# A hybrid GLA and retention trunk on one Trainium2 core: 64 and 16 bytes of slack behind each k-tile of the two activation tiles

## The chip, the cores and the metric

The kernel runs on one core of one Trainium2 chip. The metric is the device time of one execution in microseconds; smaller is better.

## What is computed

Two decoder layers on 256 tokens of width 2048, in float32: first gated linear attention (GLA, 4 heads), then multi-scale retention (8 heads). Each has a pre-RMSNorm, a wide input projection, a chunked mixer, a SiLU gate, an output projection and a residual add; a final RMSNorm ends it. Cut to the matrix work:

```
h = x
h = h + gla(rms_norm(h) )       # proj = hn @ w_in  (2048 x 10240), out = (o * silu(gate)) @ w_out (4096 x 2048)
h = h + retention(rms_norm(h))  # proj = hn @ w_in  (2048 x 12288), out = (o * silu(gate)) @ w_out (4096 x 2048)
return rms_norm(h, final_norm)
```

Nearly all the work is these four projections. Their weights, 60 groups of 2048 x 512 numbers, are read from HBM once.

## The kernel before

**Tiles.** A contraction of 2048 is cut into 16 k-tiles of 128, one k-tile on the 128 partitions. Two tiles hold activations for all 16 k-tiles: `xhl`, the normalized tokens, and `ogt`, the gated mixer outputs (half of 4096 at a time). Both have the shape `[P, NKT, 2, SEQ]`: partition, k-tile, high or low part, 256 tokens. Float32 products are made from three products of rounded numbers (high x high, high x low, low x high), so each activation and each weight is kept as a rounded high part and a rest. In a partition, one k-tile is a row of 2 x 256 x 4 = 2048 bytes, and the rows lie one behind the other.

**Weights.** `emit_raw` loads four k-tiles of a group into `raw`; `emit_split` makes the high part `hi` on ScalarE (L151) and the rest `lo` on VectorE (L152), two k-tiles at a time, two steps ahead of TensorE (`LOOK = 2`). Three buffers of `raw`, `hi` and `lo` each go round.

**Matmuls.** TensorE has a stationary operand of 128 x 128, which is loaded by a LDWEIGHTS before each matmul, and a moving operand of up to 512 columns. Two helpers use the activation tiles in two ways:

```python
def mm3(ps, lhs, kt, t, hi, lo, q):                       # in group_x: L184, L185, L186
    xh = lhs[:, kt, 0, t * P : (t + 1) * P]
    xl = lhs[:, kt, 1, t * P : (t + 1) * P]
    mm(ps, xh, hi[:, q, :], start=kt == 0, stop=False)
    mm(ps, xh, lo[:, q, :], start=False, stop=False)
    mm(ps, xl, hi[:, q, :], start=False, stop=kt == NKT - 1)
...
                    mm(ps[c], wh, rhs[:, kt, :, :], start=kt == 0, stop=False)               # in group_w: L219
                    mm(ps[c][:, 0, :], wl, rhs[:, kt, 0, :], start=False, stop=False)        # L220
```

- `group_x` (48 of the 60 groups and the tail): the activations are **stationary** (128 tokens of `xhl` or `ogt`, 512 bytes of a partition), the weights move, 512 columns. Six matmuls use one k-tile, then the next k-tile follows. Outputs named `gv`, `gg`, `rv`, `rg` read `xhl`; `ga`, `gb`, `ra`, `rb` and `tail` read `ogt`.
- `group_w` (12 groups, `gqk` and `rqk`): the weights are stationary and a row of `xhl` **moves**, 512 columns for the high weights (L219, L217) and 256 for the rest (L220, L216). Eight matmuls use one k-tile.
- In the last group (`tail`, half columns of 256), the high weights are written into the k-tile rows of `xhl`, which is no longer needed.

A few other matmuls come between: `zps` (L369, the stationary operand is 48 columns of `wa1`, whose k-tiles lie 192 bytes apart), `dg` (L507, the stationary operand is `ones_r`), `rs` (L809 to L811), `o_mms` and transposes. The order on each engine is the program's order as a scheduler at build time puts it; small work of the mixers (`side`) is fed in between the weight steps.

**Addresses.** All tiles lie in one list per partition. `smalls` is padded to 96 numbers and `ones` to 88, so that before the change `resid`, `xhl`, `ogt`, `trig`, `raw`, `hi`, `lo`, `v` and the other large working tiles start at multiples of 512 bytes, and so does every slice of them that a large matmul reads. `ones_r` is an exception: it starts 160 bytes past such a multiple.

Of the kernel before, what the change touches and what calls it, by code (L numbers as in the profile page):

```python
# [11 lines left out]
F32R = mybir.dt.float32r  # L12
# [5 lines left out]
P = 128  # L18
SEQ = 256
D = 2048  # L20
EPS = 1e-6
NKT = D // P
# [33 lines left out]
def kernel(  # L56
# [38 lines left out]
    def const(shape, name, dtype=F32):  # L95
        return one.tile(shape, dtype, tag=name, name=name)
# [152 lines left out]
    sm = const([P, 96], "smalls")[:, 0:S_N]  # L249
    ident = const([P, P], "ident")  # L250
    resid = const([P, 2, D], "resid")
    xhl = const([P, NKT, 2, SEQ], "xhl", F32R)
    ogt = const([P, NKT, 2, SEQ], "ogt", F32R)
    trig = const([P, 2, SEQ], "trig")
    rr = const([P, 2, 2], "rr")
    r2_ = const([P, 2, 2], "r2")
# [735 lines left out]
```

## Time and profile before

| | |
|---|---|
| median of 2 runs | 1416.12 us (1416.04 to 1416.2) |
| the profiled execution: its time, its span | 1417.53 us, 1415.8 us |
| TensorE matmul, weight load (share of the span) | 1403.9 us (99%), 1180.0 us (83%) |
| VectorE, ScalarE, GpSimd | 908.6 us (64%), 690.4 us (49%), 46.1 us (3%) |
| mean granted TensorE clock | 0.997 |

The span runs from the first instruction to the last one; the execution's own time is 1.73 us longer. Matmuls are pipelined: the profile gives each one a time from its start to its modelled end (389 ns for most with 512 columns), and the next one starts before that end. What counts for the total is the distance from one start to the next, which is read from the start times of a timeline. In the profile, PE is the matmul row and PEld the weight load.

### The profile page before, as it was taken

What the parts mean: (1) busy time and instruction counts of PE and PEld (TensorE: products, weight loads), DVE (VectorE), ACT (ScalarE), POOL (GpSimd) and SP (SyncE); (2) the same over time, 40 slices, a digit from 0 to 9 for tenths busy, and PEclk for the clock granted to TensorE, in tenths of its full rate; (3) what the DMA queues carried; (4) which work ended last, traced back from release to release, by engine and by line L of the source; (5) the groups of instructions that cost most, each with busy time, mean ns of one, the idle gap of its engine ahead of it and who ended that gap; (6) DMA issues with size and microseconds to landing.
All of it is one profiled execution on the core that took longest, in us unless ns stands there. A gap on an engine that the chain in (4) does not pass through costs nothing.

```text
span 1415.8 us, 17504 instructions
## 1 busy us (share of the span) xinstructions
PE 1403.9 (99%) x6800; PEld 1180.0 (83%) x6800; DVE 908.6 (64%) x1430; ACT 690.4 (49%) x889; POOL 46.1 (3%) x98
## 2 busy tenths in 40 slices
PE   8999999999999999999999999999999999999997
PEld 6888888888888888888888888888888888888887
DVE  6685796545845774665766666665556666666664
ACT  3665655534555655554444444444334444444453
POOL 0001020000010020000000000000000000000000
PEclk9999999999999999999999999999999999999999
DMA  8654555555555555555555555555555555555662
GB/s 287 240 177 149 192 180 175 183 204 180 177 179 178 188 189 179 178 178 183 190 194 192 194 189 198 179 199 181 203 182 184 196 184 199 182 203 176 209 212 94
DMA packets 40499, 266.72 MB, mean 188 GB/s; under 512 B 4880, under 2 KB 5392, under 8 KB 9696
## 3 DMA queue, kind: packets, MB, share of 16 engines
q1 hardware_dynamic: 37536, 257.57, 53.9%
q0 software_dynamic: 2160, 6.95, 1.5%
q8 instruction: 53, 0.87, 0.2%
q10 hardware_dynamic: 720, 1.09, 0.2%
q14 instruction: 30, 0.25, 0.0%
HBM read 263.49 MB, written 2.10 MB: 188 GB/s over the span
## 4 chain that ended last, share of the span: by engine, by line
PE 99%; DMA 0%; SPq 0%; DVE 0%; ACT 0%; issue 0%
PE rqk_ps L219 8%; PE gv_ps L184 4%; PE gg_ps L185 4%; PE rv_ps L184 4%; PE gv_ps L185 4%; PE gv_ps L186 4%; PE rv_ps L185 4%; PE rv_ps L186 4%; PE gg_ps L186 4%; PE gg_ps L184 4%; PE rg_ps L184 4%; PE rg_ps L185 4%; PE rg_ps L186 4%; PE rqk_ps L220 4%; PE gqk_ps L219 4%; PE gb_ps L184 2%
## 5 line engine op out<-in xcount | busy, mean ns | idle before, releaser
L152 DVE TENSOR_TENSOR lo<-raw,hi 128x1024 fp32r<-128x1024 f32 (+1 forms) x473 | 576.6, 1222 | 420.7 <-ACT hi L151 419.9
L151 ACT ACTIVATE hi<-raw 128x1024 fp32r<-128x1024 f32 (+1 forms) x473 | 499.5, 1057 | 614.4 <-PE rg_ps L186 104.6
L219 PE MATMUL rqk_ps<-xhl,hi 128*128 128x512 f32 x480 | 166.9, 398 | 0.0
L220 PE MATMUL rqk_ps<-xhl,lo 128*128 128x256 f32 x480 | 126.4, 280 | 0.0
L219 PEld LDWEIGHTS rqk_ps<-xhl,hi 128*128 128x128 f32 x480 | 88.8, 188 | 17.5
L185 PE MATMUL gg_ps<-lo,xhl 128*128 128x512 f32 x256 | 100.5, 393 | 0.0
L185 PE MATMUL gv_ps<-lo,xhl 128*128 128x512 f32 x256 | 100.4, 392 | 0.0
L185 PE MATMUL rv_ps<-lo,xhl 128*128 128x512 f32 x256 | 100.4, 392 | 0.0
L186 PE MATMUL gv_ps<-hi,xhl 128*128 128x512 f32 x256 | 100.3, 392 | 0.0
L186 PE MATMUL gg_ps<-hi,xhl 128*128 128x512 f32 x256 | 100.0, 391 | 0.0
L186 PE MATMUL rv_ps<-hi,xhl 128*128 128x512 f32 x256 | 99.7, 389 | 0.0
L185 PE MATMUL rg_ps<-lo,xhl 128*128 128x512 f32 x256 | 99.6, 389 | 0.0
L186 PE MATMUL rg_ps<-hi,xhl 128*128 128x512 f32 x256 | 99.6, 389 | 0.0
L184 PE MATMUL gv_ps<-hi,xhl 128*128 128x512 f32 x256 | 93.1, 391 | 0.0
L184 PE MATMUL rv_ps<-hi,xhl 128*128 128x512 f32 x256 | 92.1, 390 | 0.0
L220 PEld LDWEIGHTS rqk_ps<-xhl,lo 128*128 128x128 f32 x480 | 89.1, 189 | 3.4
L184 PE MATMUL rg_ps<-hi,xhl 128*128 128x512 f32 x256 | 91.8, 389 | 0.0
L184 PE MATMUL gg_ps<-hi,xhl 128*128 128x512 f32 x256 | 91.8, 391 | 0.0
L219 PE MATMUL gqk_ps<-xhl,hi 128*128 128x512 f32 x240 | 81.2, 406 | 1.6 <-ACT hi L151 1.6
L220 PE MATMUL gqk_ps<-xhl,lo 128*128 128x256 f32 x240 | 57.9, 283 | 0.5 <-DVE lo L152 0.5
L186 PEld LDWEIGHTS rv_ps<-hi,xhl 128*128 128x128 f32 x256 | 48.1, 188 | 10.0
L186 PEld LDWEIGHTS rg_ps<-hi,xhl 128*128 128x128 f32 x256 | 48.0, 188 | 10.0
(265 smaller groups left out, 2381.8 us busy)
## 6 DMA issues: line engine op xcount, KB each, us to landing
raw<-in_w_all SPq DMA_DIRECT2D x238, 1024.0 KB, 4.9
resid<-in_x_n SPq DMA_DIRECT2D x2, 1024.0 KB, 8.0
gg<-in_gn_g POOLq DMA_DIRECT2D x8, 256.0 KB, 3.8
gb<-in_gn_b POOLq DMA_DIRECT2D x8, 256.0 KB, 4.5
dm<-in_dmat POOLq DMA_DIRECT2D x8, 192.0 KB, 2.6
raw<-in_w_all SPq DMA_DIRECT2D x4, 256.0 KB, 5.0
raw<-in_w_all SPq DMA_DIRECT2D x2, 512.0 KB, 7.4
xt<-in_x_t SPq DMA_DIRECT2D x2, 512.0 KB, 8.5
```

The source lines that it names most:

```text
L151: nc.scalar.activation(hi[:, sl], src[:, sl], AF.Copy)
L152: nc.vector.tensor_tensor(lo[:, sl], src[:, sl], hi[:, sl].bitcast(F32), ALU.subtract)
L184: mm(ps, xh, hi[:, q, :], start=kt == 0, stop=False)
L185: mm(ps, xh, lo[:, q, :], start=False, stop=False)
L186: mm(ps, xl, hi[:, q, :], start=False, stop=kt == NKT - 1)
L219: mm(ps[c], wh, rhs[:, kt, :, :], start=kt == 0, stop=False)
L220: mm(ps[c][:, 0, :], wl, rhs[:, kt, 0, :], start=False, stop=False)
```

## The change

Each k-tile's row of `xhl` gets 64 bytes behind it (its stride grows from 2048 to 2112 bytes), each row of `ogt` 16 bytes (2064), and an unused tile of 256 bytes follows `ogt`:

```diff
-    xhl = const([P, NKT, 2, SEQ], "xhl", F32R)
-    ogt = const([P, NKT, 2, SEQ], "ogt", F32R)
+
+    def tokens(name, slack):
+        t = const([P, NKT, 2 * SEQ + slack], name, F32R)
+        return t[:, :, 0 : 2 * SEQ].rearrange("p k (a t) -> p k a t", a=2)
+
+    xhl = tokens("xhl", 16)
+    ogt = tokens("ogt", 4)
+    const([P, 64], "fill")
```

In the built program `xhl` starts at byte 33792 of the partition as before, `ogt` moves from 66560 to 67584, and all tiles behind it move by 1024 + 256 + 256 = 1536 bytes, three times 512: their place in a 512-byte block is what it was. So k-tile `k` of `xhl` starts 64k bytes, and that of `ogt` 16k bytes, past a multiple of 512 where both were at 0.

No instruction is added, removed or moved on any engine. The lines below the edit have numbers higher by 6. Only the splits of the last weights change their form, as they write two rows of `xhl` that no longer touch. On ScalarE, near the end of the program, the splits of weights (`hi` or `xhl` from `raw`) stand before as

```order
L151 ACTIVATE hi_10865<-raw_10767 128x1024
L151 ACTIVATE xhl<-raw_10847 128x1024 x2
L151 ACTIVATE hi_10883<-raw_10813 128x1024
L151 ACTIVATE hi_10899<-raw_10813 128x1024
L151 ACTIVATE xhl<-raw_10881 128x1024 x2
L151 ACTIVATE xhl<-raw_10915 128x1024 x2
```

and after as

```order
L151 ACTIVATE hi_10866<-raw_10768 128x1024
L151 ACTIVATE xhl<-raw_10848 128x2x512 x2
L151 ACTIVATE hi_10884<-raw_10814 128x1024
L151 ACTIVATE hi_10900<-raw_10814 128x1024
L151 ACTIVATE xhl<-raw_10882 128x2x512 x2
L151 ACTIVATE xhl<-raw_10916 128x2x512 x2
```

The rows are the same and in the same places; the 1024 numbers of one split become two runs of 512.

## The prediction

> **What bounds the kernel now.** First the page: the busy shares, the granted clock, and the chain of work that ended last.
>
> ```profile
> span 1415.8 us, 17504 instructions
> ...
> PE 1403.9 (99%) x6800; PEld 1180.0 (83%) x6800; DVE 908.6 (64%) x1430; ACT 690.4 (49%) x889; POOL 46.1 (3%) x98
> ...
> PEclk9999999999999999999999999999999999999999
> ...
> PE 99%; DMA 0%; SPq 0%; DVE 0%; ACT 0%; issue 0%
> ```
>
> The chain is TensorE from end to end at full clock; no DMA and no other engine ends a wait that matters. The time is the sum of the distances between matmul starts, so only what changes these distances counts. Next the groups of instructions by line, on PE, for how many matmuls of each kind there are:
>
> ```profile
> L219 PE MATMUL rqk_ps<-xhl,hi 128*128 128x512 f32 x480 | 166.9, 398 | 0.0
> L220 PE MATMUL rqk_ps<-xhl,lo 128*128 128x256 f32 x480 | 126.4, 280 | 0.0
> L185 PE MATMUL gg_ps<-lo,xhl 128*128 128x512 f32 x256 | 100.5, 393 | 0.0
> L185 PE MATMUL gb_ps<-lo,ogt 128*128 128x512 f32 x128 | 50.2, 392 | 0.0
> L185 PE MATMUL rb_ps<-lo,ogt 128*128 128x512 f32 x96 | 37.4, 389 | 0.0
> L185 PE MATMUL tail_ps<-tail,ogt 128*128 128x256 f32 x64 | 18.1, 283 | 0.0
> ```
>
> With `xhl` stationary there are four outputs (gv, gg, rv, rg) on three lines of 256, 3072 matmuls; with `ogt` stationary three of 3 x 128 and one of 3 x 96, 1440; the tail has 192. With `xhl` moving there are 12 groups of 64 + 64: 768 of 512 columns and 768 of 256. These 6240 of 6800 read the two changed tiles.
>
> Now the distances, from the timeline of PE (start, length, line). First a stretch of `ra`, the first and last row, with the counts of its three lines between them:
>
> ```profile
> 973.76 0.62 PE L184 MATMUL ra_ps<-hi,ogt 128*128 128x512 f32 x2
> ...
> 995.52 0.39 PE L184 MATMUL ra_ps<-hi,ogt 128*128 128x512 f32 x1
> ```
> ```profile
> L186 PE MATMUL ra_ps<-hi,ogt 128*128 128x512 f32 x32 | 12.4, 389 | 0.0
> L185 PE MATMUL ra_ps<-lo,ogt 128*128 128x512 f32 x32 | 12.4, 389 | 0.0
> L184 PE MATMUL ra_ps<-hi,ogt 128*128 128x512 f32 x32 | 11.2, 389 | 0.0
> ```
>
> 96 matmuls in 995.52 - 973.76 = 21.76 us: **226.7 ns** each, every one with the same 389 ns length. I call this the steady beat. The tail does the same with 256 columns:
>
> ```profile
> 1399.84 0.28 PE L185 MATMUL tail_ps<-tail,ogt 128*128 128x256 f32 x1
> ...
> 1401.88 0.28 PE L184 MATMUL tail_ps<-xhl,ogt 128*128 128x256 f32 x1
> ```
>
> 17 steps (a row each 0.12 us) in 2.04 us, 120 ns. The 256 columns more cost 226.7 - 120 = 106.7 ns, so 512 columns stream in 213.3 ns and each matmul has 13.3 ns on top, whatever its length. This excess is the only thing that an address could change.
>
> **Is the excess a collision of the weight load with the moving operand?** Look at a matmul beside which no weight load ran (timelines of PEld and of PE):
>
> ```profile
> 59.81 0.19 PEld L184 LDWEIGHTS gg_ps<-hi,xhl 128*128 128x128 f32 x1
> 60.35 0.33 PEld L395 LDWEIGHTS rb<-dg,ones 128*16 128x16 f32 x4 [0.35 <-issue]
> ```
> ```profile
> 60.04 0.39 PE L184 MATMUL gg_ps<-hi,xhl 128*128 128x512 f32 x1
> ```
>
> It streamed from 60.04 on; the next load began 0.31 us later, yet its length is 0.39 us as ever. So in the steady beat the loads cost the stream hardly anything: the aligned addresses are already without collisions, and staggering them has little to take away. Lengths track distances, and over the whole run they hardly go below the steady ones (the answers by source line, min/median/max ns):
>
> ```profile
> L184 PE MATMUL gg_ps<-hi,xhl x256: 387/389/476, 58.0 to 579.5; 128*128 128x512 f32 x128
> L219 PE MATMUL rqk_ps<-xhl,hi x480: 387/395/477, 670.9 to 1270.9; 128*128 128x512 f32 x160
> L220 PE MATMUL rqk_ps<-xhl,lo x480: 274/280/285, 671.4 to 1271.1; 128*128 128x256 f32 x160
> ```
>
> With `xhl` stationary the median sits 2 ns above the minimum; with `xhl` moving, 395 and 280 stand 8 and 6 above.
>
> **What a stationary address off the 512-byte grid costs.** Two places of this run show it. `dg` loads `ones_r`, 160 bytes off the grid, four times:
>
> ```profile
> 75.14 0.40 PE L186 MATMUL gg_ps<-hi,xhl 128*128 128x512 f32 x1
> 75.38 0.64 PE L507 MATMUL dg<-qkp,ones_r 128*128 128x256 f32 x4
> 75.86 0.62 PE L184 MATMUL gg_ps<-hi,xhl 128*128 128x512 f32 x2
> ...
> 77.25 0.39 PE L184 MATMUL gg_ps<-hi,xhl 128*128 128x512 f32 x1
> ```
>
> The matmul beside which the first such load runs takes 0.24 us, the four of 256 columns 0.12 each, and the six that follow 77.25 - 75.86 = 1.39 us, 232 ns each, before the beat is back. From 75.14 to 77.25 it is 2.11 us where the steady beat makes 7 x 0.2267 + 4 x 0.12 = 2.07: some 0.04 us for two changes of address, there and back, about **20 ns a change**. And `zps` steps its stationary address by 192 bytes each time:
>
> ```profile
> 21.23 2.94 PE L369 MATMUL zps<-xhl,wa 128*48 128x512 f32 x12
> 24.02 0.62 PE L219 MATMUL gqk_ps<-xhl,hi 128*128 128x512 f32 x2
> ```
>
> Twelve in 2.79 us, 232.5 ns: with a step each time the beat is never found, 5.8 ns a matmul.
>
> But a break needs no odd address: one matmul of another length does it too, with all operands on the grid.
>
> ```profile
> 705.47 0.28 PE L809 MATMUL rs<-rqs,rks 128*128 128x256 f32 x1
> 705.58 0.63 PE L184 MATMUL rv_ps<-hi,xhl 128*128 128x512 f32 x2
> ...
> 706.97 0.39 PE L184 MATMUL rv_ps<-hi,xhl 128*128 128x512 f32 x1
> ```
>
> 0.11 us, then six in 1.39: 1.50 against 0.12 + 6 x 0.2267 = 1.48, again 0.02 us lost. So the beat is a rhythm that TensorE falls into and that any irregular step breaks for about six matmuls.
>
> The Trainium skill speaks against any effect: in "TensorE: Matmul & The Clock Gate", section "Step-by-step: what each phase is for", it gives TensorE two independent read ports, so that loading the next weights takes nothing from the running matmul. By that rule the sum is zero and the time 1416.1 us. The trace agrees in the steady beat (0.39 us with and without a load) and disagrees beside `ones_r` (0.24 us instead of 0.2267).
>
> **The sum.** No instruction is added or moved; the eight splits of changed form run on ScalarE, 49% busy, under the tail's matmuls, and cost nothing unless they doubled: one takes about as long as any other split,
>
> ```profile
> L151 ACT ACTIVATE xhl<-raw 128x1024 fp32r<-128x1024 f32 x8 | 8.0, 1052 | 4.3 <-DMA raw<-in_w_all 4.3
> ```
>
> and eight more microseconds of ScalarE would still fit there. What remains is the break at each new k-tile of the stationary operand: 32 groups x 16 = 512 steps of 64 bytes on `xhl`, 15 x 16 = 240 of 16 bytes on `ogt`. No row here has a step of 16 or 64 bytes under 128-column loads. Bounds: nothing (each such step is absorbed), or 20 ns each, 752 x 0.02 = 15 us, and if the beat is never found again, 5.8 ns x 4512 = 26 us. Below nothing: the minima allow 2 ns x 4512 = 9 us, and 8 x 768 + 6 x 768 ns = 11 us where `xhl` moves, since there the rows are off the beat now and the new residues may put them on it; all together 20 us.
>
> The nearest row is the 160-byte one, and I scale its price with the size of the step, an estimate: 20 x 64/160 = 8 ns x 512 = 4.1 us, and 20 x 16/160 = 2 ns x 240 = 0.5 us; for `xhl` moving, tail and the rest, zero between their ends. The sum is +4.6 us on the profiled execution's 1417.53, which lies 1.41 above the median: 1417.53 + 4.6 - 1.41 = 1420.7 us, **1421**. That is +0.3%; a run of this kernel tells about 2% from no change for a verdict.
>
> **The rivals.**
> - *No effect*, 1416 us: steps in whole 64 or 16 bytes keep the phase. For it: the beat is the same at all multiples of 512. Chance 0.20.
> - *The beat is lost*, the slower side: a 64-byte step counts as much as `ones_r`'s. Place: each first matmul of a k-tile in gv, gg, rv, rg. Price between 15 us (a break each) and 26 us (never found, as in `zps`): 1431 to 1442, say 1436. It decides from the point where six matmuls, one k-tile's worth, don't suffice to find the beat. Against it: `zps` has 48-column loads and stood off the beat before. Chance 0.19.
> - *The stagger helps*: rows where `xhl` moves fall nearer their minima, and stationary ones gain 1 to 2 ns: half of the 20 us to all of it, 1396 to 1406, say 1404. For it: L219's 395 against 387. Against it: nothing in the trace shows a new residue doing that. Chance 0.19.
> - *The 13.3 ns are themselves a collision that staggering ends*: taking half of it from 4512 + 1536 matmuls saves 6.65 x 6048 = 40 us, 1376. Against it: the matmul without a load. Chance 0.05. The same page of the skill, in "Back-to-back issue gap", has N/2.4 + 2.5 ns for a warm matmul, an estimate of 215.8 ns here; no run here shows it, 226.7 is measured.
>
> **How the numbers follow.** The forecast, a small loss or none to speak of (1417 to 1428), has 0.37; with the rivals that is 1. Range: the largest part of both middle rivals, 1398 to 1440. Faster by over 2% (below 1387.8): the fourth rival and a little of the third, 0.06. Slower by over 2% (above 1444.4): what lies beyond the second one's end, if moving rows get worse too, 0.05. Within: 0.89.
>
> **What would show it.** In the profile after: the stretch of `ra` at 226.7 ns a matmul and 389 ns on every row says that 16-byte steps are absorbed; a median of gv, gg, rv, rg above 389, or maxima of 395 to 398 every six matmuls, that 64-byte steps break the beat; near 395 throughout, that it is lost. L219 and L220 below 395 and 280 is the third rival. All medians well under 387 would make the prediction wrong: then loads and stream do collide at equal residues. An unchanged profile at another time, or a span lost outside PE, would make it wrong in another way.

## The result, and the profile after

The changed kernel takes **1436.54 us** (median of 2 runs, 1435.76 to 1437.32) against 1416.12 us: a ratio of 1.0144, with a 95% interval of 1.0101 to 1.0188. It is slower by some 20 us, 1.4%, and the whole interval lies above 1. The profiled execution took 1437.32 us. All times below are medians over a kernel's executions; one execution far out of line, 3659.68 us of the first experiment's kernel, moves that median from 1441.56 to 1441.72 us and is left out of its ratio.

First the page of the changed kernel: span, busy shares, granted clock, and the chain that ended last.

```profile
span 1435.5 us, 17504 instructions
...
PE 1423.0 (99%) x6800; PEld 1181.0 (82%) x6800; DVE 909.8 (63%) x1430; ACT 690.4 (48%) x889; POOL 45.4 (3%) x98
...
PEclk9999999999999999999999999999999999999999
...
PE 99%; DMA 0%; ACT 0%; SPq 0%; DVE 0%; issue 0%; ACTq 0%
```

The chain is TensorE from end to end as before, at the same clock, with as many instructions on every engine. The span grew by 1435.5 - 1415.8 = 19.7 us, PE's busy time by 1423.0 - 1403.9 = 19.1 us; the other engines moved by about 1 us or less. The time went into the matmuls themselves. The groups by line show which (PE rows; the last two numbers ahead of the idle time are busy us and mean ns):

```profile
L219 PE MATMUL rqk_ps<-xhl,hi 128*128 128x512 f32 x480 | 167.1, 397 | 0.0
L220 PE MATMUL rqk_ps<-xhl,lo 128*128 128x256 f32 x480 | 126.9, 281 | 0.0
L185 PE MATMUL gg_ps<-lo,xhl 128*128 128x512 f32 x256 | 101.6, 397 | 0.0
```

Where `xhl` moves, nothing happened in sum: 397 and 281 ns, 398 and 280 before. Where it is stationary, as in `gg`, a matmul is 4 ns longer: 397 against 393. The two answers below are for one of the three `mm3` lines (L186), first of the kernel before, then of the changed one; the columns are minimum, median and maximum ns, and the first and last start.

```profile
L186 PE MATMUL rg_ps<-hi,xhl x256: 389/389/389, 717.8 to 1318.2; 128*128 128x512 f32 x128
L186 PE MATMUL rb_ps<-hi,ogt x96: 389/389/479, 1319.1 to 1385.6; 128*128 128x512 f32 x96
```
```profile
L186 PE MATMUL rg_ps<-hi,xhl x256: 388/394/398, 728.1 to 1337.0; 128*128 128x512 f32 x128
L186 PE MATMUL rb_ps<-hi,ogt x96: 387/394/479, 1337.9 to 1405.7; 128*128 128x512 f32 x96
```

Before, all 256 matmuls of `rg` on this line had 389 ns, the steady beat without an exception. After, the median is 394 in both, so the 16-byte steps on `ogt` cost as much per matmul as the 64-byte steps on `xhl`.

The timeline of PE in the changed kernel shows where in `ra` the beat is lost (start, length; six matmuls use one k-tile, counted from the group's beginning; the residue is the place of the stationary address past a multiple of 256 bytes, and the weights are at 0):

```profile
976.59 0.63 PE L184 MATMUL ra_ps<-hi,ogt 128*128 128x512 f32 x2
...
977.99 0.39 PE L184 MATMUL ra_ps<-hi,ogt 128*128 128x512 f32 x1
...
986.34 0.39 PE L184 MATMUL ra_ps<-hi,ogt 128*128 128x512 f32 x1
...
987.70 0.62 PE L184 MATMUL ra_ps<-hi,ogt 128*128 128x512 f32 x2
...
990.19 0.40 PE L186 MATMUL ra_ps<-hi,ogt 128*128 128x512 f32 x1
990.43 0.62 PE L184 MATMUL ra_ps<-hi,ogt 128*128 128x512 f32 x2
...
991.82 0.40 PE L184 MATMUL ra_ps<-hi,ogt 128*128 128x512 f32 x1
```

- From 976.59 to 977.99 the k-tile at residue 128: six matmuls in 1.40 us, 233 ns each. It doesn't settle within the k-tile.
- From 986.34 the k-tile at 240, from 987.70 the one at 0 (the next group begins), then the one at 16 up to 990.19: 17 matmuls in 3.85 us, 226.5 ns. **Through two steps of 16 bytes the beat holds.**
- The matmul at 990.19 still has a stationary operand at residue 16, yet takes 0.24 us. What runs beside it is the load of the next one, the first at residue 32. From 990.43 on, at 32, six take 1.39 us, 232 ns.

The same holds over all of `ga`, `gb`, `ra` and `rb`: by the starts in PE's timeline, the k-tiles at residues 240, 0 and 16 take 226.8, 227.5 and 228.4 ns a matmul on average, the other thirteen 229.6 to 233.7 (where the next matmul of the same output starts within 300 ns).

So it seems to be the load running beside a matmul whose address counts, and what counts need not be that the address has changed: some residues keep the beat and others don't. That leaves three theories. **A, the difference:** a matmul is on the beat when the load beside it and its own moving operand stand at nearly the same place modulo 256 bytes. **B, the step** (the prediction's): any change of residue breaks the beat for some six matmuls. **C, the grid:** addresses off the 512-byte grid are slow in themselves.

### The profile page after: what moved, and what is told of

Same layout as the page of the kernel before. It is cut to its first block, busy times and chain, and to the rows that moved or that the text cites. A ratio compares the mean times of both kernels' runs of the same rounds, so it can differ in the third digit from the quotient of the medians.

```text
span 1435.5 us, 17504 instructions
## 1 busy us (share of the span) xinstructions
PE 1423.0 (99%) x6800; PEld 1181.0 (82%) x6800; DVE 909.8 (63%) x1430; ACT 690.4 (48%) x889; POOL 45.4 (3%) x98
## 4 chain that ended last, share of the span: by engine, by line
PE 99%; DMA 0%; ACT 0%; SPq 0%; DVE 0%; issue 0%; ACTq 0%
PE rqk_ps L219 8%; PE gg_ps L185 4%; PE gv_ps L184 4%; PE rv_ps L184 4%; PE gv_ps L185 4%; PE rg_ps L185 4%; PE rv_ps L185 4%; PE gg_ps L184 4%; PE rg_ps L184 4%; PE rv_ps L186 4%; PE gv_ps L186 4%; PE rg_ps L186 4%; PE gg_ps L186 4%; PE rqk_ps L220 4%; PE gqk_ps L219 4%; PE gb_ps L184 2%
## 5 line engine op out<-in xcount | busy, mean ns | idle before, releaser
L186 PE MATMUL gv_ps<-hi,xhl 128*128 128x512 f32 x256 | 101.3, 396 | 0.0
L186 PE MATMUL gg_ps<-hi,xhl 128*128 128x512 f32 x256 | 101.0, 395 | 0.0
L186 PE MATMUL rv_ps<-hi,xhl 128*128 128x512 f32 x256 | 100.8, 394 | 0.0
L186 PE MATMUL rg_ps<-hi,xhl 128*128 128x512 f32 x256 | 100.7, 393 | 0.0
L185 PEld LDWEIGHTS rg_ps<-lo,xhl 128*128 128x128 f32 x256 | 48.1, 188 | 11.3
L186 PEld LDWEIGHTS rg_ps<-hi,xhl 128*128 128x128 f32 x256 | 48.2, 188 | 11.0
```

## The experiments

Each diff is against the kernel before, cut to the lines that matter; `tokens` is the function that the change brings in. Where a tile behind is pushed, padding brings the tiles behind it to the grid again unless the diff says otherwise.

**Both token tiles shifted by 128 bytes, no step.**

```diff
+    const([P, 32], "ahead")
     xhl = const([P, NKT, 2, SEQ], "xhl", F32R)
     ogt = const([P, NKT, 2, SEQ], "ogt", F32R)
+    const([P, 96], "behind")
```

> No slack, so no k-tile differs from another; both token tiles as a whole stand 128 bytes off the 512-byte grid, the weights on it. Theory A (what counts is where the stationary address stands against the moving one, modulo 256 bytes; steps don't matter): all 4512 matmuls with xhl or ogt stationary go as those of residue 128 do in the changed kernel, where the rows of ra alternate 229 and 238 ns: 4512 x about 6.5 ns = +29 us, 1445 us, slower than the staggered kernel. Theory B (a change of residue breaks the beat for some six matmuls, as the prediction had it): there is no change, the beat holds at 226.7 ns, 1416 us. Theory C (every address off the 512-byte grid is slow in itself): 1445 us as A.

Measured: 1441.72 us, ratio 1.0174 (1.0154 to 1.0195). No k-tile differs from another, and the loss is 25.3 us where the stagger lost 20.4 (the intervals of the two ratios overlap). L186 by source line:

```profile
L186 PE MATMUL rg_ps<-hi,xhl x256: 390/392/404, 729.7 to 1341.3; 128*128 128x512 f32 x128
L186 PE MATMUL rb_ps<-hi,ogt x96: 390/393/478, 1342.3 to 1410.3; 128*128 128x512 f32 x96
```

The minimum is 390: of these 256 matmuls of `rg` not one has the 389 ns of the beat. Theory B alone is out. The size is 25.3 us and not the 29 expected: over 4512 matmuls that is 5.6 ns each, where the rows of `ra` had suggested 6.5.

**The weights shifted by 128 instead of the token tiles.**

```diff
     ogt = const([P, NKT, 2, SEQ], "ogt", F32R)
+    const([P, 32], "fill")          # everything behind: 128 bytes off the grid
```

> No slack; the token tiles on the grid, the split weights and all tiles behind them 128 bytes off it. Theory A (the difference counts, whichever side is shifted): as with the token tiles shifted by 128 alone, about 1445 us. Theory B (steps): 1416 us. A theory by which only the stationary address counts: 1416 us.

Measured: 1443.11 us, 1.0183 (1.0166 to 1.0200), with the same lengths:

```profile
L186 PE MATMUL rg_ps<-hi,xhl x256: 390/393/405, 731.2 to 1342.9; 128*128 128x512 f32 x128
```

Here every stationary token slice is on the grid. So it isn't the stationary address alone. Which side is shifted doesn't matter at 128 bytes, where ahead and behind are the same modulo 256.

**Everything shifted by 128.**

```diff
+    const([P, 32], "ahead")
     sm = const([P, 96], "smalls")[:, 0:S_N]
```

> No slack; 128 bytes ahead of all large tiles, so that token tiles and weights stand off the 512-byte grid by the same 128 bytes. Theory A (stationary against moving): the difference is zero again, beat 226.7 ns, 1416 us. Theory B (steps): 1416 us. Theory C (off the grid is slow in itself): as with the token tiles alone, 1445 us.

Measured: 1416.41 us, 1.0000 (0.9991 to 1.0009).

```profile
L186 PE MATMUL rg_ps<-hi,xhl x256: 389/389/389, 716.0 to 1316.4; 128*128 128x512 f32 x128
```

Both operands are off the grid and the beat is there for all 256. Theory C is out; the difference counts.

**Steps of 256 bytes.** Residues 0 and 256 modulo 512 in turn (even k-tiles, slack, odd k-tiles):

```diff
+    class Tokens:                       # k-tile kt at [kt % 2][kt // 2]
+            t = const([P, 2, NKT // 2 * 2 * SEQ + 64], name, F32R)
...
+            return self.v[(p, kt // 2, kt % 2, *rest)]
+    xhl = Tokens("xhl")
+    ogt = Tokens("ogt")
```

> The k-tiles of both token tiles alternate between residues 0 and 256 modulo 512: the even ones lie together, then 256 bytes of slack, then the odd ones. Theory A (modulo 256): 256 counts as zero, the beat holds through every step, 226.7 ns, 1416 us. Theory B (each of 752 steps breaks the beat, 20 ns each): +15 us, 1431 us. Theory A with a period of 512 bytes instead: half of the k-tiles off the beat, +13 to +15 us, 1430 us.

Measured: 1416.04 us, 0.9996 (0.9987 to 1.0005).

```profile
L186 PE MATMUL rg_ps<-hi,xhl x256: 389/389/389, 716.0 to 1316.4; 128*128 128x512 f32 x128
```

752 steps of 256 bytes cost nothing, and every matmul of `rg` on this line has 389 ns as before: 256 bytes count as zero, 128 don't, so the period is 256 bytes, and a change of address as such breaks no beat.

The Trainium skill, "TensorE: Matmul & The Clock Gate", section "Step-by-step: what each phase is for", says that the load has a read port of its own and takes no read bandwidth from the running matmul. By that rule these four runs would agree; they lie 27 us apart and differ in addresses alone, so here the measurement decides. What inside the chip has the period of 256 bytes no run shows.

**The two slacks apart.**

```diff
+    xhl = tokens("xhl", 16)      # 64 bytes; the other run: 0
+    ogt = tokens("ogt", 0)       # the other run: 4, 16 bytes
```

> Only the 64-byte slack on xhl; ogt as before. The prediction's sum: 8 ns x 512 steps, +4.1 us, 1420 us. Theories A and B alike, by the rows of the changed kernel (gv, gg, rv, rg 231.4 to 231.6 ns instead of 226.7 to 227.5, 3072 matmuls): +13 us, 1429 us, and ga, gb, ra, rb back at 226.7 ns.

> Only the 16-byte slack on ogt; xhl as before. The prediction's sum: 2 ns x 240 steps, +0.5 us, 1416.6 us. By the rows of the changed kernel (231.4 ns instead of 226.9, 1440 matmuls): +6.5 us, 1422.6 us. Together with the run that has the slack on xhl alone it should add up to the whole change, +20 us.

Measured: 1429.40 us, 1.0091 (1.0076 to 1.0106), with the slack on `xhl`; 1422.15 us, 1.0040 (1.0025 to 1.0055), with that on `ogt`. Against the 1416.22 us beside them that is +13.2 and +5.9, together +19.1 of the change's +20.4. L186 of the first run and then of the second:

```profile
L186 PE MATMUL rg_ps<-hi,xhl x256: 388/394/398, 723.4 to 1330.5; 128*128 128x512 f32 x128
L186 PE MATMUL rb_ps<-hi,ogt x96: 387/389/479, 1331.4 to 1398.0; 128*128 128x512 f32 x96
```
```profile
L186 PE MATMUL rg_ps<-hi,xhl x256: 389/389/389, 720.1 to 1322.2; 128*128 128x512 f32 x128
L186 PE MATMUL rb_ps<-hi,ogt x96: 387/394/479, 1323.1 to 1390.9; 128*128 128x512 f32 x96
```

Of the outputs with stationary tokens, each slack hits those that read its own tile and no others. A step costs 13.2 / 512 = 26 ns with 64 bytes and 5.9 / 240 = 25 ns with 16.

**A quarter of the step on xhl.**

```diff
+    xhl = tokens("xhl", 4)       # 16 bytes
+    ogt = tokens("ogt", 0)
```

> Slack on xhl alone, 16 bytes instead of 64: residues 0, 16, ... 240. The prediction's price in proportion to the step: 2 ns x 512, +1 us, 1417 us. Theory A (the residue against the weights counts, 3 of 16 residues keep the beat): 3072 x (231.4 - 227.0) = +13.5 us, 1429.6 us, as much as 64-byte steps. Theory B (each step breaks it): 512 x 20 ns = +10 us, 1426 us.

Measured: 1431.13 us, 1.0102 (1.0087 to 1.0117): 14.9 us, with 16-byte steps no less than with 64-byte ones.

**How wide is the window? A constant 16 and a constant 240 bytes.**

```diff
+    def shifted(name):
+        t = const([P, NKT * 2 * SEQ + 64], name, F32R)
+        t = t[:, 4 : 4 + NKT * 2 * SEQ]        # 16 bytes; the other run: 60, 240 bytes
+        return t.rearrange("p (k a t) -> p k a t", a=2, t=SEQ)
...
+    xhl = shifted("xhl")
+    ogt = shifted("ogt")
```

Each tile grows by 256 bytes, so `ogt` starts at another 256 past the grid in both runs; modulo 256 the two tiles agree.

> No slack; both token tiles as a whole stand 16 bytes off the grid. Theory A, with the window that the changed kernel's ra rows show (beat held at 240, 0 and 16, lost at 32): 1416 us, 226.7 ns. Theory B: 1416 us. Theory C: anything from 1416 us (in proportion to the offset) to 1445 us.

Measured: 1433.03 us, 1.0114 (1.0099 to 1.0129). This was a miss, since all three residues had held the beat in the rows of `ra` above. L186 again, three outputs:

```profile
L186 PE MATMUL rg_ps<-hi,xhl x256: 390/395/398, 725.8 to 1333.2; 128*128 128x512 f32 x128
L186 PE MATMUL ga_ps<-hi,ogt x128: 394/394/397, 255.2 to 345.2; 128*128 128x512 f32 x128
L186 PE MATMUL ra_ps<-hi,ogt x128: 389/389/483, 963.1 to 1050.3; 128*128 128x512 f32 x128
```

`ga` and `ra` are the same work on the same tile at the same residue. `ra` is mostly on the beat, and `ga` never is on this line: its minimum is 394. At 16 bytes two rhythms can go on. PE's timeline of this run shows one change from the beat to the other:

```profile
708.55 0.39 PE L184 MATMUL rv_ps<-hi,xhl 128*128 128x512 f32 x1
...
709.91 0.62 PE L184 MATMUL rv_ps<-hi,xhl 128*128 128x512 f32 x2
710.36 0.60 PE L813 MATMUL rs<-ra 128*128 128x128 f32 x4
...
711.04 0.40 PE L186 MATMUL rv_ps<-hi,xhl 128*128 128x512 f32 x1
...
712.44 0.39 PE L184 MATMUL rv_ps<-hi,xhl 128*128 128x512 f32 x1
```

Before the four small matmuls of `rs`, six take 709.91 - 708.55 = 1.36 us, 227 ns each; after them, six take 712.44 - 711.04 = 1.40 us, 233 ns each, and `rv` doesn't come back. In this run every change from one rhythm to the other that lasts five matmuls or more stands next to matmuls of another output; in between, the rhythm stays what it was. So what came before decides which one a group is in; what in it decides isn't shown. I looked at the other side next:

> As the run at 16 bytes, with the token tiles as a whole at residue 240 (16 bytes short of 256) against the weights. Both residues held the beat in the rows of ra of the changed kernel, but at a constant 16 the beat held in ra (226.7 ns) and was lost in rg (233.3). Theory: the window is one-sided; 240 also brings a lost beat back (rows of 240 follow those of 224 in the changed kernel at 226.9 ns): gv, gg, rv, rg at 227 ns, 1414 to 1418 us. Rival: the window is symmetrical, and 240 loses it in part like 16, 1430 us.

Measured: 1418.51 us, 1.0016 (1.0007 to 1.0025).

```profile
L186 PE MATMUL rg_ps<-hi,xhl x256: 389/389/390, 719.4 to 1321.0; 128*128 128x512 f32 x128
L186 PE MATMUL ga_ps<-hi,ogt x128: 387/392/397, 254.3 to 342.5; 128*128 128x512 f32 x128
L186 PE MATMUL ra_ps<-hi,ogt x128: 387/390/478, 953.7 to 1041.3; 128*128 128x512 f32 x128
```

Here `rg` is on the beat throughout. `ga` and `ra` are not, but they lose little. A group of 96 in `ra`, from its first row to the next group's first:

```profile
997.67 0.62 PE L184 MATMUL ra_ps<-hi,ogt 128*128 128x512 f32 x2
...
1019.59 0.62 PE L184 MATMUL ra_ps<-hi,ogt 128*128 128x512 f32 x2
```

That is 21.92 us, 228.3 ns a matmul, 1.6 above the beat; a group of `ga` at 16 bytes (278.23 to 300.63 in that run's timeline) took 233.3. The window is one-sided: a stationary address 16 bytes behind the moving one costs a seventh of one 16 bytes ahead (2.3 us against 16.6). Of the constant differences tried, 0, 16, 128 and 240, only 0 was without loss.

**The stagger kept, the weights staggered with it.** 32 bytes on `xhl`, and the split weights start at the residue of their k-tile:

```diff
+            step = 0 if i // NSUB in OUT else 8
+            off = i % NSUB * SUB * step % 64
...
+                t = pool.tile([P, SUB * GW + 64], F32R, tag=tag, name=f"{tag}{i}")
+                t = t[:, off : off + SUB * (GW + step)] if step else t[:, 0 : SUB * GW]
...
+    xhl = tokens("xhl", 8)
```

> The stagger kept and its harm taken out: 32 bytes of slack on xhl, and the split weights of every group that works with xhl start at the same residue as their k-tile, so that within a k-tile stationary and moving address always agree modulo 256; ogt without slack. Only the load of a new k-tile's first weights runs beside the last matmul of the old k-tile, 32 bytes apart. Theory A: the beat returns within each k-tile; 512 steps at nothing to 20 ns, 1416 to 1426 us, below the 1429 to 1431 us of unmatched slack on xhl alone. Theory that the steps themselves cost: 1429 us or more, as without the match.

Measured: 1425.60 us, 1.0063 (1.0046 to 1.0079); its kernel before took 1417.48. One k-tile of `rg` and the first row of the next in PE's timeline:

```profile
864.83 0.62 PE L191 MATMUL rg_ps<-hi,xhl 128*128 128x512 f32 x2
865.29 0.39 PE L192 MATMUL rg_ps<-lo,xhl 128*128 128x512 f32 x1
865.51 0.39 PE L193 MATMUL rg_ps<-hi,xhl 128*128 128x512 f32 x1
865.74 0.39 PE L192 MATMUL rg_ps<-lo,xhl 128*128 128x512 f32 x1
865.97 0.40 PE L193 MATMUL rg_ps<-hi,xhl 128*128 128x512 f32 x1
866.20 0.39 PE L191 MATMUL rg_ps<-hi,xhl 128*128 128x512 f32 x1
```

After the first row, three distances of 0.22 or 0.23 us up to 865.97; the last matmul is 0.40 long, and beside it runs the load of the next k-tile, 32 bytes off. This k-tile is a good one: its six take 1.37 us, 228.3 ns each. Over all of `gv`, `gg`, `rv` and `rg` in this run, by the starts in PE's timeline, the first and the last of the six take 231.0 and 233.6 ns on average and the four between them 226.1 to 231.5, so the beat comes back within a k-tile only in part. By the ratio, 0.0063 x 1416 = 8.9 us over 512 steps is 17 ns a step (the medians, 8.1 us apart, give 16). That is less than 16-byte slack without the match; against the 64-byte one the intervals just touch (1.0079 and 1.0076). So the loss of a stagger can be read as two parts that fit these numbers: a break at each new k-tile and what follows it, some 17 ns, and the rest of the 25 ns, because the beat isn't found while the difference lasts. No run separates the two; slack of 32 bytes without the match was not run.

**Can a difference help where xhl moves?** The two lengths alternate there (512 and 256 columns) and the 389 ns of the beat aren't the rule even before (median 395); at a constant 16 these pairs had been faster. So only the weights of the query-key groups were shifted:

```diff
+QK = (0, 5, 14, 19, 28, 31, 34, 37, 44, 47, 50, 53)
...
+            off = 60 if i // NSUB in QK else 0           # 240 bytes; the other run: 56, 224
...
```

> Aims below the kernel before: the weights of the twelve query-key groups alone (stationary there, xhl moving, 512 and 256 columns in turn) start 16 bytes short of 256, so that the moving residue is 16 ahead of the stationary one there; all other groups stay at difference zero. In the run at a constant 16 the pair of 512 and 256 columns took 347.9 ns instead of 349.8, 768 pairs: -1.4 us, 1414.8 us. Rival: the gain there was of another cause or is not repeated: 1416.2 us.

> The same with 32 bytes. In the run with 16-byte slack on xhl the 28 pairs at difference 32 took 345.2 ns on average, in passing from one residue to the next; if it holds for all 768 pairs, -3.5 us, 1412.7 us; if it was only the passage, as at residues around it (349.6 to 351.9), 1416 us or up to 1418 us.

Measured: 1416.37 us, 0.9996 (0.9987 to 1.0005), and 1416.41 us, 0.9995 (0.9986 to 1.0003). The 512-column matmuls of `rqk` (16, then 32 bytes; in both kernels the line is L224):

```profile
L224 PE MATMUL rqk_ps<-xhl,hi x480: 388/392/482, 670.5 to 1269.9; 128*128 128x512 f32 x160
```
```profile
L224 PE MATMUL rqk_ps<-xhl,hi x480: 390/390/484, 668.7 to 1267.9; 128*128 128x512 f32 x160
```

The median fell from 395 to 392 and 390; by the starts in PE's timeline all of `rqk` gained 0.5 and 0.9 us in the two profiled executions. No gain in the kernel's time can be told from zero. The step from 347.9 and 345.2 ns a pair to a sum was too hopeful. No version here beats the kernel before.

## Why the prediction was right in part

The time lies inside the range (1398 to 1440), but only because the range was drawn to hold the largest part of two rivals as well. Of the cases it was not the forecast of 1421 that came, but the rival "the beat is lost" (chance 0.19). That it came within 1 us of the 1436 given there is luck: 1436 is the middle between two prices for steps of the address, 15 and 26 us, and a step as such is not the cause.

- **The bound: right.** PE ends the time, nothing else moved. The eight splits of changed form take what they took, 1054 ns against 1052 (changed kernel, ScalarE's groups by line):

```profile
L151 ACT ACTIVATE xhl<-raw 128x1024 fp32r<-128x1024 f32 x8 | 8.0, 1054 | 3.6 <-DMA raw<-in_w_all 3.6
```

- **Aligned addresses have nothing to gain: right for 512 columns.** In no run did an output with stationary tokens and 512 columns get a median under 389. The rivals "the stagger helps" and "the 13.3 ns are a collision" needed that. The row offered as evidence beforehand is weaker: the 0.39 us of the matmul without a load beside it is a modelled end, with no next start close behind to check it.
- **The beat, and that a break costs about 20 ns: right in size.** The run with matched weights, where a difference is left only at the k-tile boundaries, shows some 17 ns a step.
- **The step that failed: the price scaled with the size of the step.** The prediction took 8 ns for 64 bytes and 2 ns for 16; measured were 26 and 25. It had +4.1 and +0.5 us where the runs show +13.2 and +5.9, and for 16-byte steps on `xhl` the same rule gives 1 us against 14.9. Nothing in the trace of before supported a proportion. The unscaled bounds that stood beside it, 15 us for a break at each step and 26 us if the beat is never found, enclose the measured 20.
- **The rule behind it was wrong too.** The step was taken as the cause. Steps of 256 bytes cost nothing, and 128 bytes without any step cost 25 us. `zps` and `ones_r` fit the difference as well: steps of 192 bytes run through differences 64 bytes apart, and the matmul beside the first load of `ones_r` has a difference of 160. The prediction read both as changes of address. The signs that it named for the changed kernel did tell the case: `ra` is off 226.7 ns (231.4 on average by the starts), and the medians with stationary tokens stand at 392 to 394, above 389 and near the 395 of a lost beat.
- **Where xhl moves: zero, as taken.** 397 and 281 ns against 398 and 280.

## What to carry to other kernels

When matmuls like these (a load of 128 x 128 for each, 512 columns) follow each other without a gap, place the stationary and the moving operand at the same address modulo 256 bytes, in every k-tile. A common shift of 128 bytes was free, and shifting one side alone by 128 bytes cost this kernel 1.7 to 1.8%. Of the steps between k-tiles tried here, 16, 32, 64 and 256 bytes, only 256 was harmless. And when a trace shows a regular beat, don't scale the price of its loss with the size of the disturbance: steps of 16 bytes cost as much as steps of 64, and the unscaled bounds held.

## What was not expected of the hardware

- A sixteenth of the 256-byte period is enough to lose the beat, on one side far more than on the other. At 16 bytes ahead the same work runs at 227 or at 233 ns a matmul, and keeps to either until other matmuls come between.
- The 256-column matmuls of the tail are *shorter* with the stagger. First the kernel before, then the changed one:

```profile
L185 PE MATMUL tail_ps<-tail,ogt x64: 274/283/283, 1379.4 to 1407.4; 128*128 128x256 f32 x64
```
```profile
L185 PE MATMUL tail_ps<-tail,ogt x64: 276/280/288, 1399.4 to 1427.2; 128*128 128x256 f32 x64
```

  The median is 280 ns instead of 283, and the tail's matmuls start 118.1 ns apart on average instead of 119.8. So what is best for 512 columns need not be best for 256.
- What makes the period of 256 bytes, and why the excess of 13.3 ns per matmul stays at best, is open; no run touched it. Nor does any run show what the matmuls would do without a load beside them.
